# A decoder layer on one core: M's load on another queue, a new order inside the DeltaNet heads, later conditioning sums

## The chip, the cores and the metric

The kernel runs on 1 core of one Trainium2 chip. The metric is the device time of that core in microseconds (us). Names of the engines: PE is TensorE (matmuls; PEld its weight loads), DVE is VectorE, ACT is ScalarE, POOL is GpSimd, SP is SyncE. Each engine works through its own instructions in order, and they meet through semaphores. SP, ACT and POOL also issue DMA transfers, each in its own order.

## What is computed

One layer of a decoder over 1024 positions of width 1024, all in fp32. A conditioning vector `c` gives six vectors by one product with `w_ada`; a projection feeds sliding-window attention (16 query heads, 4 key heads, window 128, sinks) and a gated DeltaNet (8 heads of 128) in parallel. Both are gated, merged and projected, and a squared-ReLU MLP of width 4096 follows.

```python
mod = c_act @ w_ada[l] + b_ada[l]
sh1, sc1, gt1, sh2, sc2, gt2 = jnp.split(mod[:, None, :], 6, axis=-1)
u = x * (1.0 + sc1) + sh1
proj = u @ w_in[l]
qa, ka, va, dq, dk, dv, z, b_raw, a_raw, g_a, g_b = _split_in(proj)
y_a = _sliding_window_attention(qa, ka, va, sinks[l]) @ w_oa[l]
y_b = _gated_deltanet(dq, dk, dv, z, b_raw, a_raw, conv_w[l], a_log[l], dt_bias[l], dn_norm_w[l]) @ w_ob[l]
mixed = (jax.nn.sigmoid(g_a) * y_a + jax.nn.sigmoid(g_b) * y_b) @ w_out[l]
x = _layer_norm(ALPHA * x + (1.0 + gt1) * mixed, ln1_g[l], ln1_b[l])
u2 = x * (1.0 + sc2) + sh2
h = jnp.square(jax.nn.relu(u2 @ w_ff1[l] + b_ff1[l]))
x = _layer_norm(ALPHA * x + (1.0 + gt2) * (h @ w_ff2[l] + b_ff2[l]), ln2_g[l], ln2_b[l])
```

Inside a DeltaNet head the state goes from chunk to chunk (with `o` divided by its RMS and multiplied with `silu(z)` at the end; q, k and v first pass a convolution of 4 taps and a silu):

```python
v_new = u_c - jnp.einsum('bhck,bhkv->bhcv', w_c, state)
o_c = jnp.einsum('bhck,bhkv->bhcv', q_c, state) + jnp.einsum('bhcs,bhsv->bhcv', intra_c, v_new)
state = state * last_c[..., None, None] + jnp.einsum('bhck,bhcv->bhkv', k_c, v_new)
```

The triangular system of each chunk of 64 (`I + L`, one for every head and chunk, 128 in all) is the matrix M of the kernel.

## The kernel before

**The stream.** Almost all time is one stream of matmuls of 128x512 on PE. An fp32 product is made of three products of fp32r parts: high by high, high by low, low by high. `split_s` makes the parts: ACT copies the high part (L215), DVE subtracts it to get the low part (L216). `stream_unit` computes 128 output columns for all 1024 positions: 2 halves of 8 k tiles of 3 products, 48 matmuls (L248). Each takes one *position*, and `count[0]` is the current one.

**What sets the order.** Everything else is tied to positions by hand: `at(p, f)` puts an event into a heap and `after(n, f)` puts it n positions on; before each matmul of the stream `run_events` fires what is due. An event may issue a matmul, a DVE or ACT instruction or a DMA. So PE, DVE and ACT run in exactly the order of these numbers. The DMA issues of SP and POOL are placed by the same events, but their order within these two queues is set by a scheduler from what the transfers wait for.

**Stage b** is 26 units (keys, queries, gates) up to position Q0 = 1248. The 64 attention slots run in it: `att_scores` (L803, L804) multiplies the queries `qs` with the keys `khh` and `kll`. `k_parts` makes those: ACT copies a half tile (L747), DVE subtracts (L752), and each half is copied to the other 64 partitions by a DMA of POOL's queue (L748, L753). In the same stage DVE solves the triangular systems. They come from DRAM as M, 2 MB (L683, on POOL's queue, issued ahead of the keys' copies); `solve_init` (L686) sets the diagonal at position SOL0, and 124 steps (L701, L706) are spread up to SOL1 = 1150.

**The head stage** has 8 heads of 144 positions, each with a unit for q, for v and for z. After the unit of q or v, ACT copies the product to `pad` (L952) and scales it (L953), DVE adds three taps (L956) and ACT applies the silu (L961). A unit of z ends in two silus to `sz` (L1202). The recurrence of a head runs beside the next head's units, eight chunks n = 0 to 7, in hops of 6 positions: `hd_a` (PE L1127, then DVE rhs L1129), `hd_b` (PE L1137, then ACT vn L1139), `hd_c` (PE L1147, then DVE St L1152; PE L1160, then ACT Square L1163 and DVE o copy L1164). After it `hd_norm` takes the Sqrt on ACT (L1172) and scales the eight chunks of o, and `hd_out` transposes them and multiplies with `sz` (L1192). E products (L1101) and v products (L1115, L1119) of a head are made ahead of its recurrence, which starts at R = b + 140, b being the head's first position (b + 168 for head 7).

**The conditioning sums.** The remaining four vectors of `mod` are made by DVE from 68 loads of 256 KB or a row of the bias, `ada_load`, issued on SP; `ada_add` (L993, L995) adds each to an accumulator, and `ada_part` closes each of the 8 sums with matmuls.

**Then** the attention output is loaded (`attn_load`) and split (`attn_split`) during the last unit of z, two projections with their gates follow (`ya_done` takes the sigmoid of a gate tile), the output mix (L1469), the layer norm, and the MLP (L1840, L1900).

## Time and profile before

| | |
|---|---|
| median of 3 runs (lowest to highest) | 1851.2 us (1850.14 to 1852.37) |
| the profiled execution | 1854.92 us, span 1853.2 us |
| granted clock of the profiled execution | 0.992 |
| busy share PE / PEld / DVE / ACT / POOL | 98 / 81 / 69 / 55 / 17 % |
| DMA, mean over the span | 182 GB/s |

The profiled execution is one run, 3.7 us above the median; a sum made from its rows stands against its own time. In rows of the profile a line number leads to the code above, `x` is a count, and what stands in brackets is the idle time of the engine just before the instruction with what ended it. A window row has a stretch, its length, each engine's busy time, the granted clock of PE (1.00 is full), the share of the DMA engines and GB/s. A busy PE is not a PE at full rate: matmuls of 0.39 us overlap, one starting every 0.23 us.

### The profile page before, as it was taken

The numbers are of one execution on the slowest core, as the hardware profiler recorded it, in microseconds if no ns is written. First come the engines' busy times: TensorE is split into PE (matmuls) and PEld (weight loads), VectorE is DVE, ScalarE is ACT, GpSimd is POOL, SyncE is SP. The second block draws the span as 40 slices with busy tenths as digits, with TensorE's granted clock in tenths as the row PEclk, the third lists the DMA queues.
The fourth block names the chain that finished last, engine by engine and source line by source line (L and its number), as shares of the span: only waits on it lengthen the run. The fifth ranks groups of instructions, "written<-read, shape, count | busy, mean of one in ns | idle before, by whom it ended". The sixth has DMA issues, their size and how long they took to land.

```text
span 1853.2 us, 26168 instructions
## 1 busy us (share of the span) xinstructions
PE 1817.6 (98%) x9161; PEld 1505.5 (81%) x9161; DVE 1281.0 (69%) x2405; ACT 1022.8 (55%) x2297; POOL 314.4 (17%) x465
## 2 busy tenths in 40 slices
PE   8999999999999999999999999999999999999997
PEld 6977788888887888888878888877788887888886
DVE  6687588988855666666554445788767676576697
ACT  4698578888874454554554322465555555434341
POOL 0233233444331000000001110002212120000000
PEclk8999999999999999999999999999999999999999
DMA  9655622232257454444445644359887879755571
GB/s 276 200 199 202 197 89 85 61 99 80 81 195 203 144 154 136 141 143 139 119 156 199 192 153 151 117 169 314 306 277 264 268 250 389 274 183 182 199 256 46
DMA packets 262670, 337.74 MB, mean 182 GB/s; under 512 B 26261, under 2 KB 171366, under 8 KB 262282
## 3 DMA queue, kind: packets, MB, share of 16 engines
q1 hardware_dynamic: 223210, 212.94, 36.5%
q0 software_dynamic: 31328, 108.44, 17.4%
q10 hardware_dynamic: 8000, 14.68, 2.2%
q8 instruction: 72, 1.18, 0.2%
q14 instruction: 60, 0.49, 0.1%
HBM read 231.40 MB, written 102.51 MB: 180 GB/s over the span
## 4 chain that ended last, share of the span: by engine, by line
PE 80%; DVE 6%; ACT 4%; DMA 4%; issue 2%; POOL 0%; SPq 0%; ACTq 0%; DVEq 0%; POOLq 0%
PE mm L248 34%; PE mm L1840 7%; PE mm L1900 6%; PE b L1900 4%; PE a L1900 4%; PE b L1840 3%; PE a L1840 2%; PE mm L1469 2%; PE c L1900 2%; PE c L878 1%; PE a L1469 1%; PE mm L188 1%; PE mm L187 1%; PE mm L186 1%; PE a L1137 1%
## 5 line engine op out<-in xcount | busy, mean ns | idle before, releaser
L248 PE MATMUL mm<-uh,wl 128*128 128x512 f32 x800 | 332.7, 416 | 0.0
L248 PE MATMUL mm<-ul,wh 128*128 128x512 f32 x800 | 322.2, 403 | 0.0
L248 PE MATMUL mm<-uh,wh 128*128 128x512 f32 x800 | 319.0, 399 | 0.0
L216 DVE TENSOR_TENSOR sp<-sraw,sp 128x1024 fp32r<-128x1024 f32 x112 | 132.8, 1220 | 77.3 <-ACT sp L215 77.2
L215 ACT ACTIVATE sp<-sraw 128x1024 fp32r<-128x1024 f32 x112 | 112.7, 1054 | 123.0 <-PE b L1900 75.4
L248 PEld LDWEIGHTS mm<-ul,wh 128*128 128x128 f32 x800 | 151.6, 189 | 26.6 <-issue 0.2
L248 PEld LDWEIGHTS mm<-uh,wl 128*128 128x128 f32 x800 | 152.2, 190 | 23.1 <-issue 4.0
L248 PEld LDWEIGHTS mm<-uh,wh 128*128 128x128 f32 x800 | 152.4, 191 | 21.5 <-issue 0.2
L1900 PE MATMUL mm<-sp 128*128 128x512 f32 x528 | 136.9, 390 | 1.1 <-DVE sp L216 1.1
L1900 PEld LDWEIGHTS mm<-sp 128*128 128x128 f32 x528 | 98.5, 188 | 22.0 <-DVE sp L216 1.8
L216 DVE TENSOR_TENSOR wl<-wr,wh 128x1024 fp32r<-128x1024 f32 x81 | 99.9, 1234 | 8.9 <-ACT wh L215 8.8
L215 ACT ACTIVATE wh<-wr 128x1024 fp32r<-128x1024 f32 x81 | 85.1, 1051 | 21.4 <-PE c L1469 14.1
L1900 PE MATMUL a<-sp 128*128 128x512 f32 x336 | 92.6, 390 | 0.0
L1139 ACT ACTIVATE vn<-a,brk 128x128 f32<-128x128 f32 x64 | 23.5, 367 | 108.4 <-PE a L1137 107.4
L1900 PE MATMUL b<-sp 128*128 128x512 f32 (+1 forms) x336 | 80.0, 374 | 0.0
L811 DVE CUSTOM_DVE_ANT_0 nscore<-a,amask,nsink 128x256 f32<-128x256 f32 (+1 forms) x128 | 54.6, 464 | 36.5 <-PE a L804 35.8
L863 POOL TENSOR_SCALAR_AFFINE_SELECT pl<-ph 128x512 fp32r<-128x512 f32 x56 | 64.6, 1154 | 76.3 <-DVE ph L856 59.0
L1900 PEld LDWEIGHTS a<-sp 128*128 128x128 f32 x336 | 63.1, 188 | 13.1
L1900 PEld LDWEIGHTS b<-sp 128*128 128x128 f32 x336 | 60.5, 188 | 11.2
L216 DVE TENSOR_TENSOR wl<-fraw,wh 128x1024 fp32r<-128x1024 f32 x43 | 52.6, 1223 | 22.7 <-ACT wh L215 22.4
L822 POOL TENSOR_TENSOR sm<-sm 128x256 f32<-128x256 f32 x56 | 48.5, 866 | 95.7 <-ACT sm L818 53.1
L818 ACT ACTIVATE sm<-nscore,stat 128x257 f32<-128x257 f32 (+1 forms) x128 | 61.9, 486 | 2.7 <-DVE stat L811 2.5
(522 smaller groups left out, 4654.9 us busy)
## 6 DMA issues: line engine op xcount, KB each, us to landing
wr<-in_w_in_dram SPq DMA_DIRECT2D x60, 512.0 KB, 3.6
sraw<-hf_d SPq DMA_DIRECT2D x54, 512.0 KB, 4.3
adaw<-in_w_ada_dram SPq DMA_DIRECT2D x73, 256.0 KB, 4.6
fraw<-in_w_ff_dram SPq DMA_DIRECT2D x32, 512.0 KB, 5.5
sraw<-wt_d SPq DMA_DIRECT2D x32, 512.0 KB, 4.5
hf_d<-t ACTq DMA_DIRECT2D x48, 256.0 KB, 4.0
wt_d<-wx POOLq DMA_DIRECT2D x48, 256.0 KB, 3.0
sraw<-in_w_ff_dram SPq DMA_DIRECT2D x22, 512.0 KB, 5.5
```

The source lines that it names most:

```text
L186: T.matmul(t, lhsT=wh[:, k, :], rhs=xh[k][:, sl], start=k == 0, stop=False)
L215: A.activation(out=hi, in_=src, func=AF.Copy)
L216: after(lag, lambda: V.tensor_tensor(out=lo, in0=src, in1=hi.bitcast(F32), op=ALU.subtract))
L248: T.matmul(ts[half], lhsT=w[:, k, :], rhs=xx[k][:, sl], start=k == 0 and m == 0, stop=k == KT - 1 and m == 2)
L811: V.tensor_tensor_reduce(out=ns[:, i, 1:1 + W], in0=sc[:, i * 2 * P:i * 2 * P + W], in1=amask[:, mo:mo + W], scale=-1.0, scalar=nsink[:, 2 ...
L818: A.activation(out=sm[:, i, 0:1 + W], in_=ns[:, i, 0:1 + W], func=AF.Exp, scale=-1.0, bias=st[:, i:i + 1], accum_out=st[:, 2 + i:3 + i])
L822: G.tensor_tensor(out=sm[:, :, 1 + P:1 + 2 * P], in0=sm[:, :, 1:1 + P], in1=sm[:, :, 1 + P:1 + 2 * P], op=ALU.add)
L863: G.affine_select(out=flat4(part), in_=flat4(full), pattern=[[0, 4], [1 if odd else -1, P]], compare_op=ALU.is_ge if odd else ALU.is_gt, f ...
L1139: after(1, lambda: A.activation(out=vn, in_=Wp[:, 0:P], func=AF.Copy, scale=brk[:, n, h:h + 1]))
L1469: T.matmul(pt, lhsT=m[k][:, tok], rhs=w[:, k % 2, :], start=k == 0 and w is wh and m is mh, stop=k == KT - 1 and m is ml)
L1840: T.matmul(pt, lhsT=a[:, k0 + k, :], rhs=b[k], start=begin and k == 0 and x_ == 0, stop=k == 3 and x_ == 2, skip_group_check=True)
L1900: T.matmul(to, lhsT=a[:, f, t * P:(t + 1) * P], rhs=b[:, f, lo:up], start=(begin or own) and s % NS == 0 and f == 0 and x_ == 0, stop=s % ...
```

## The change

It has these parts.

1. M is loaded by a DMA of ACT's queue, issued 18 positions after the key unit's end, instead of POOL's queue ahead of the keys' copies. The solve starts at position 192 instead of 164 and ends at 1150 as before.
2. Conditioning item i is loaded at Q0 + 170 + 13 i instead of Q0 + 21 + 14 i, added 28 positions later instead of 21, and the sums of the last four close at +35 instead of +28. The first three loads still leave SP ahead of the head's loads.
3. In the head stage the taps and their silu come one position later; the copy of o on DVE comes 9 positions after its hop instead of 4 (the Square stays at 4); odd chunks of o are scaled on ACT in all heads instead of only the last; the norm of heads 0 to 5 comes 2 positions after the recurrence instead of 8, with `hd_out` at +18 and +21 instead of +19 and +24 after it; head 6's `hd_out` moves to +25 and +36. In head 0 the transposes of q and v come 10 and 8 positions later.
4. Three of the eight attention splits move by 4 to 12 positions, behind the last unit's two silus. The first gate's sigmoid comes 38 positions after its load instead of 20.

```diff
@@ -680,7 +680,9 @@
...
     Mf = M.rearrange("p s c -> p (s c)")
-    nc.gpsimd.dma_start(out=Mf, in_=md_d.rearrange("h b n s c -> (h b n) (s c)"))
+
+    def solve_load():
+        nc.scalar.dma_start(out=Mf, in_=md_d.rearrange("h b n s c -> (h b n) (s c)"))
 
@@ -714,7 +716,7 @@
...
 
-    SOL0, SOL1 = 164, 1150
+    SOL0, SOL1 = 192, 1150
     cost = [s * (63 - s) + 80 for s in range(1, 63)]
@@ -908,6 +910,7 @@
...
     at(KEY0 + 17, k_parts, 0, 1)
+    at(KEY0 + 18, solve_load)
     at(max(slot(15) + 1, 48 * (units_b.index(("k", 1)) + 1) + 4), k_parts, 1, 0)
@@ -957,8 +960,8 @@
...
             for j in range(3):
-                after(4 + 4 * j, tap, 2 - j)
-            after(16, lambda: A.activation(out=dst[:, sl], in_=dst[:, sl], func=AF.Silu))
+                after(5 + 4 * j, tap, 2 - j)
+            after(17, lambda: A.activation(out=dst[:, sl], in_=dst[:, sl], func=AF.Silu))
         return done
@@ -981,11 +984,11 @@
...
             nc.sync.dma_start(out=w, in_=w_ada[k * P:(k + 1) * P, lo:lo + HALF])
-            after(21, ada_add, w, k)
+            after(28, ada_add, w, k)
         else:
...
         if k == KT - 1 + (f < 4):
-            after(28, ada_part, f, w[0:1, :])
+            after(28 if f < 4 else 35, ada_part, f, w[0:1, :])
 
@@ -1024,7 +1027,7 @@
...
     for i, (f, k) in enumerate(items):
-        at(Q0 + 21 + 14 * i, ada_load, i, f, k)
+        at(Q0 + 170 + 13 * i, ada_load, i, f, k)
 
@@ -1159,10 +1162,8 @@
...
 
-        def put():
-            A.activation(out=junk(), in_=op_[:, 0:P], func=AF.Square, accum_out=d["sso"][:, n:n + 1])
-            V.tensor_copy(out=d["o"][:, cs], in_=op_[:, 0:P])
-        after(4, put)
+        after(4, lambda: A.activation(out=junk(), in_=op_[:, 0:P], func=AF.Square, accum_out=d["sso"][:, n:n + 1]))
+        after(9, lambda: V.tensor_copy(out=d["o"][:, cs], in_=op_[:, 0:P]))
 
@@ -1174,7 +1175,7 @@
...
                 V.reciprocal(out=fs, in_=fs)
-            if h == 7 and n % 2:
+            if n % 2:
                 A.activation(out=d["o"][:, chunk(n)], in_=d["o"][:, chunk(n)], func=AF.Copy, scale=fs[:, n:n + 1])
@@ -1208,9 +1209,9 @@
...
         for half in range(2):
-            at(b + 58 + 24 * half, hd_qturn, h, half)
+            at(b + (58 if h else 68) + 24 * half, hd_qturn, h, half)
             at(max(b + 64, late + 40) + 24 * half, hd_kq, h, half)
-            at(b + 98 + 24 * half, hd_vturn, h, half)
+            at(b + (98 if h else 106) + 24 * half, hd_vturn, h, half)
         at(max(b + 70, late + 50), hd_z, h)
@@ -1218,10 +1219,10 @@
...
             at(R + 3 * HOP * n + 2 * HOP, hd_c, h, n)
-        late = R + 3 * HOP * NT + (14 if h == 6 else 8)
+        late = R + 3 * HOP * NT + (14 if h == 6 else 8 if h == 7 else 2)
         at(late, hd_norm, h)
-        at(late + 19, hd_out, h, 0)
-        at(late + 24, hd_out, h, 1)
+        at(late + (25 if h == 6 else 19 if h == 7 else 18), hd_out, h, 0)
+        at(late + (36 if h == 6 else 24 if h == 7 else 21), hd_out, h, 1)
 
@@ -1245,14 +1246,14 @@
...
                 at(count[0] + (0, 0, 0, 26, 36, 32, 38, 44)[k], attn_load, k)
-                at(count[0] + (8, 14, 20, 38, 43, 50, 56, 62)[k], attn_split, k)
+                at(count[0] + (8, 14, 20, 38, 55, 50, 60, 66)[k], attn_split, k)
         stream_unit(uh, ul, sz_done(h), interleave=h == 7)
...
         nc.gpsimd.dma_start(out=t, in_=ga_d[f])
-        after(20, lambda: A.activation(out=t, in_=t, func=AF.Sigmoid))
+        after(20 if f else 38, lambda: A.activation(out=t, in_=t, func=AF.Sigmoid))
 
```

How this moves instructions, at three places. In the rows a line number of the changed kernel is up to 3 above that of the kernel before.

The first is the start of attention on POOL's queue, before and after. M is the matrix of systems, khh and kll are the keys' parts.

```order
L599 DMA e_d<-e 128x1024
L683 DMA M<-md_d 128x4096
L748 DMA khh<-khh 64x512
L753 DMA kll<-kll 64x512
L748 DMA khh<-khh 64x512
```

```order
L599 DMA e_d<-e 128x1024
L750 DMA khh<-khh 64x512
L755 DMA kll<-kll 64x512
L750 DMA khh<-khh 64x512
L755 DMA kll<-kll 64x512
```

The keys' copies now follow the last store directly; the load of M (L685) stands on ACT, behind the third copy of khh (L749) and ahead of a weight split (L215) and the fourth copy.

The second is the hop n = 2 on DVE, here that of head 2, from the state St to the next rhs, before and after. `ada` is the conditioning accumulator, `wl` a weight's low part, `sz` the product of `hd_out`.

```order
L1152 SCALAR_TENSOR_TENSOR St<-St,last,a 128x128
L956 SCALAR_TENSOR_TENSOR qT<-pad,convc,qT 128x512
L995 SCALAR_TENSOR_TENSOR ada<-ada,c_col 128x512
L216 TENSOR_TENSOR wl<-wr,wh 128x1024
L1164 COPY o<-c 128x128
L1192 SCALAR_TENSOR_TENSOR sz<-b,convc,sz 128x512
L956 SCALAR_TENSOR_TENSOR qT<-pad,convc,qT 128x512
L1129 SCALAR_TENSOR_TENSOR rhs<-a,negegc,vr 128x128
```

```order
L998 SCALAR_TENSOR_TENSOR ada<-adaw,c_col,ada 128x512
L1155 SCALAR_TENSOR_TENSOR St<-St,last,a 128x128
L216 TENSOR_TENSOR wl<-wr,wh 128x1024
L959 SCALAR_TENSOR_TENSOR qT<-pad,convc,qT 128x512
L1132 SCALAR_TENSOR_TENSOR rhs<-a,negegc,vr 128x128
L959 SCALAR_TENSOR_TENSOR qT<-pad,convc,qT 128x512
```

One tap, the conditioning add, the copy of o and the product to `sz` no longer stand between St and rhs.

The third is the boundary between two heads on ACT, here from head 1 to head 2: Square of the last chunk (`junk,sso`), silu of the second half of `sz`, vn of the next head's first chunk, and the Sqrt of the norm (`fs`), before and after.

```order
L1163 ACTIVATE junk,sso<-c 128x128
L1202 ACTIVATE sz<-mm 128x512
L1139 ACTIVATE vn<-a,brk 128x128
L1172 ACT_TABLE_LOAD
L1172 ACTIVATE fs<-fs,eps_q 128x8
L1163 ACTIVATE junk,sso<-c 128x128
L1139 ACTIVATE vn<-a,brk 128x128
```

```order
L1165 ACTIVATE junk,sso<-c 128x128
L1173 ACT_TABLE_LOAD
L1173 ACTIVATE fs<-fs,eps_q 128x8
L1203 ACT_TABLE_LOAD
L1203 ACTIVATE sz<-mm 128x512
L1142 ACTIVATE vn<-a,brk 128x128
L1179 ACTIVATE o<-o,fs 128x128 x4
L1165 ACTIVATE junk,sso<-c 128x128
L1142 ACTIVATE vn<-a,brk 128x128
```

The Sqrt with its table load, and a second table load for the silu, now stand ahead of the silu and of vn; the table load that the next silu needed before (at L961, a few rows on) is gone. Four scalings of o follow vn.

## The prediction

> **What bounds the kernel now.** I read the page first: who is busy, and what the chain that ended last is made of.
>
> ```profile
> PE 1817.6 (98%) x9161; PEld 1505.5 (81%) x9161; DVE 1281.0 (69%) x2405; ACT 1022.8 (55%) x2297; POOL 314.4 (17%) x465
> PE 80%; DVE 6%; ACT 4%; DMA 4%; issue 2%; POOL 0%; SPq 0%; ACTq 0%; DVEq 0%; POOLq 0%
> ```
>
> PE is busy for 98% of the span. The change removes no matmul, so it can only win what PE loses by standing still or by running at a lower clock. The next view is the list of PE's waits: who waits, for whom, then us in total, times, longest.
>
> ```profile
> PE a L1137 <- DVE rhs L1129: 4.2, 7, 1.0
> PE b L1115 <- DVE E L1101: 2.4, 1, 2.4
> PE a L803 <- DMA M<-md_d: 2.3, 1, 2.3
> ```
>
> These three are the longest in the list and all lie in code that the diff touches. Two are a single wait each, so I looked at the granted clock around them (stretch: its length, busy time of PE, PEld, DVE, ACT, POOL, then clock, DMA share, GB/s).
>
> ```profile
> 226.20:229.00 2.80, 0.51 (x3) 0.12 (x2) 0.75 (x4) 0.00 (x0) 0.42 (x1) 1.00 1.39 226
> 230.70:234.20 3.50, 3.50 (x10) 2.73 (x9) 3.33 (x11) 1.25 (x4) 0.00 (x0) 0.51 0.84 201
> 575.50:578.40 2.90, 0.48 (x4) 0.09 (x2) 2.61 (x7) 1.16 (x3) 0.00 (x0) 1.00 1.12 268
> 578.90:582.40 3.50, 3.50 (x11) 2.74 (x10) 1.51 (x3) 1.85 (x6) 0.56 (x1) 0.52 0.99 224
> 1303.50:1305.40 1.90, 0.43 (x2) 0.00 (x1) 0.00 (x0) 0.60 (x2) 0.00 (x0) 1.00 0.84 326
> ```
>
> Each of the two long gaps (2.3 and 2.4 us idle) is followed, some 2 us and 0.5 us later, by 3.5 us at a clock of 0.51 and 0.52: 3.5 × 0.49 = 1.7 us of work lost each time. The gap of 1.5 us at 1303.5 leaves no such mark in its own stretch. I charge both stretches to their gaps.
>
> A gap costs a little more than its idle time, because matmuls of the stream overlap:
>
> ```profile
> 692.69 0.40 PE L248 MATMUL mm<-ul,wh 128*128 128x512 f32 x1
> 692.92 0.39 PE L1147 MATMUL a<-vn,kd 128*128 128x128 f32 x2
> ...
> 226.25 0.39 PE L248 MATMUL mm<-uh,wh 128*128 128x512 f32 x1
> 228.93 0.30 PE L803 MATMUL a<-khh,qs 128*128 128x128 f32 x1 [2.29 <-DMA M<-md_d]
> ```
>
> A matmul of 0.40 is followed by the next start after 0.23. At 226.25 the next comes after 2.68, so 2.45 is lost where 2.29 is shown idle: 0.16 more per gap.
>
> **Edit 1, M's load.** The wait at 228.93 is put down to M, but the first score matmul reads khh, kll and qs. Its half copies khh and kll go out on POOL's queue behind M.
>
> ```profile
> 216.81 0.55 POOL L683 DMA_DIRECT2D M<-md_d  x1 [7.74 <-DVE kll L752]
> ...
> M<-md_d POOLq DMA_DIRECT2D x1, 2048.0 KB, 11.2
> khh<-khh POOLq DMA_DIRECT2D x4, 128.0 KB, 11.8
> ...
> DMA to landing us min/median/max: 2.2/2.4/3.1
> ...
> 228.16 0.11 DVE L686 MEMSET M<- 128x64 f32 x1 [5.39 <-DMA M<-md_d]
> ```
>
> M takes 11.2 us from issue to landing; a khh copy behind it takes 11.8 at the median, and the four later ones (second row of landings, of the tile khh from 300 to 480 us) 2.4. With M on ACT's queue after the third khh copy, the copies go out at about 217 and would land some 3 to 6 us later, before 226.5. The gap goes: −2.45, and with it its half-clock stretch, −1.7; together **−4.1**. ACT pays one issue, priced by this row:
>
> ```profile
> 1283.02 0.33 ACTq L1553 DMA_DIRECT2D hf_d<-t  x1
> ```
>
> It stands ahead of a weight split and the last khh copy; 0.33 late is covered by ACT's slack there (in the 2.80 us stretch at 226.20 ACT ran nothing). What is late next is M: issued near 217 it lands at 228.2 by its own 11.2. The solve's memset now stands 28 positions later (28 × 0.23 = 6.4 us), near 228.8 in a stream without the gap, behind the first score's maximum on DVE. If M were as slow as the slowest load below (14.7), DVE would stand until 231.8, and everything queued behind the memset with it: the first attention slots' maxima, then PE. Bounds of this edit: −4.1 and 0 (the wait only changes its name). I take −4.1, nearer to M's own row. The solve has 28 of 986 positions less; DVE is 69% busy, so at nothing.
>
> **Edit 2, the conditioning sums.** The wait at 578 has this history (first row from the chain of waits, second from DVE's timeline):
>
> ```profile
> 561.03 14.73 DMA ada<-in_w_ada_dram
> ...
> 577.12 1.12 DVE L1101 SCALAR_TENSOR_TENSOR E<-b,rk,E 128x128 f32<-128x128 f32 x4
> ```
>
> A conditioning load of 256 KB lands 14.7 us after issue, because it shares the queues with the head loads; the add waits for it on DVE, the E products stand behind the add, and PE's L1115 waits for those. Loads from the fourth on now come 149 positions (34 us) later, after the head loads, and their adds 28 instead of 21 positions behind. The wait goes: 2.42 + 0.16 = −2.6, and −1.7 for the clock: **−4.3**; bounds −4.3 and −2.6, or 0 if another load there is as late. What is given back is below, since all 68 items now end at Q0 + 170 + 13 × 67 = Q0 + 1041, close to the last head.
>
> **Edit 3, the hop that waits.** All seven waits of L1137 are the same hop, n = 2 of heads 0 to 6. This is the one of head 2 (DVE's timeline, then PE's):
>
> ```profile
> 698.85 0.35 DVE L1152 SCALAR_TENSOR_TENSOR St<-St,last,a 128x128 f32<-128x128 f32 x1 [0.16 <-PE a L1147]
> 699.37 0.75 DVE L956 SCALAR_TENSOR_TENSOR qT<-pad,convc,qT 128x512 f32<-128x512 f32 x1 [0.17 <-ACT qT L953]
> 700.04 0.75 DVE L995 SCALAR_TENSOR_TENSOR ada<-ada,c_col 128x512 f32<-128x512 f32 x1
> 700.70 1.22 DVE L216 TENSOR_TENSOR wl<-wr,wh 128x1024 fp32r<-128x1024 f32 x1
> 701.84 0.29 DVE L1164 COPY o<-c 128x128 f32<-128x128 f32 x1
> 702.04 0.74 DVE L1192 SCALAR_TENSOR_TENSOR sz<-b,convc,sz 128x512 f32<-128x512 f32 x1
> 702.70 0.74 DVE L956 SCALAR_TENSOR_TENSOR qT<-pad,convc,qT 128x512 f32<-128x512 f32 x1
> 703.36 0.35 DVE L1129 SCALAR_TENSOR_TENSOR rhs<-a,negegc,vr 128x128 f32<-128x128 f32 x1
> ...
> 703.76 0.49 PE L1137 MATMUL a<-rhs,TT 128*128 128x128 f32 x2 [1.04 <-DVE rhs L1129]
> ```
>
> Between St and rhs DVE is 4.51 us on work of others, and PE waits 1.04. After the change only the weight subtraction (start to start 1.14) and one tap (0.66) stand between them: the conditioning add (0.66), the o copy (0.20), the gated product (0.66) and one tap have moved elsewhere. That is 0.52 + 1.14 + 0.66 = 2.3 us, 2.2 less where 1.04 was short; the other six hops lack the add and have more room. All seven go: 4.2 + 7 × 0.16 = −5.3. The pieces land in neighbouring hops; counted over the new order with these durations the fullest of these holds 2.9 us, and hops with 3.1 run without a wait today. I take **−5.2**; bounds −5.3 and 0 (work merely moved).
>
> **Edit 4, the last head and the attention splits.**
>
> ```profile
> 939.12 1.15 ACT L215 ACTIVATE ah<-ar 128x512 fp32r<-128x512 f32 x2 [2.19 <-DMA ar<-attn_d]
> 940.17 1.07 ACT L1202 ACTIVATE sz<-mm 128x512 f32<-128x512 f32 x2
> ...
> 940.80 0.50 PE L248 MATMUL mm<-ah,wh 128*128 128x512 f32 x1 [1.29 <-ACT sz L1202]
> 951.09 0.49 PE L1147 MATMUL a<-vn,kd 128*128 128x128 f32 x2 [0.60 <-ACT vn L1139]
> ```
>
> PE waits for the silu because two ah copies that wait for their load stand before it; after the change the silu stands first. That wait goes: −1.29 − 0.16 = −1.45. The one at 951 and two of 0.3 to 0.4 behind it keep most of their cause: ACT has the same copies plus four scalings there. I take **−2.0**; bounds −1 and −3.2 (all four).
>
> **What is given back.** Six head boundaries (heads 0 to 5) get a longer chain on ACT: last Square, table load, Sqrt, table load, silu of the second sz half, then vn, for which PE waits. Before, the Sqrt came behind vn:
>
> ```profile
> 688.91 0.20 ACT L1163 ACTIVATION_READ_ACCUMULATOR junk<-c 128x1 f32 x1
> 691.05 0.60 ACT L1202 ACTIVATE sz<-mm 128x512 f32<-128x512 f32 x1 [1.95 <-PE mm L248]
> 691.80 0.37 ACT L1139 ACTIVATE vn<-a,brk 128x128 f32<-128x128 f32 x1
> 692.18 1.28 ACT L1172 ACT_TABLE_LOAD   x1
> 693.48 0.30 ACT L1172 ACTIVATE fs<-fs,eps_q 128x8 f32<-128x8 f32 x1
> ```
>
> The Square ends at 689.11 and PE's L1147 starts without a wait at 692.92 (its row is above): 3.81 us. The chain is 1.30 + 0.30 + 1.30 + 0.60 + 0.37 = 3.87, so 0.06 per head. If the second load starts only with the silu's input (691.05), vn ends at 691.05 + 1.30 + 0.60 + 0.37 = 693.32: 0.40 per head, 2.4 in all. I take **+0.4**, between them but near the first, because the load at 692.18 began without waiting for the Sqrt's input. The Trainium skill speaks against this edit: "ScalarE: Activation LUTs", section "What ACT_TABLE_LOAD costs", gives about 1.28 us for a load and 1.38 more for a drain at each switch; the trace agrees on 1.28, but its Sqrt starts 0.02 us behind its load, so the drain isn't seen here.
>
> The rest, **+0.7** (0 to +2.5): the conditioning sums now run beside the last heads and the attention loads, whose buffers come free only when the sums end, and the gate's sigmoid is moved; the nearest rows are waits of 0.3 to 1.3 at single places.
>
> **The sum.** −4.1 − 4.3 − 5.2 − 2.0 + 0.4 + 0.7 = −14.5 from the profiled execution's own 1854.9 us, so 1840.4. That execution lies 3.7 us above the median of the runs (1851.2), which I take to stay with the profile: **1836.7 us**. If every loss named here went and nothing came back it would be −4.1 − 4.3 − 5.3 − 3.2 = −16.9, or 1834.3.
>
> **Rivals.** *The half-clock stretches are not the gaps'.* At 1303.5 a gap has none, and one comes 2 us behind its gap. Then both stay somewhere: +3.4, 1840.1. The Trainium skill leans this way ("TensorE: Matmul & The Clock Gate", "What's actually happening"): the clock falls after an idle window of about 3.4 us, and no gap here is that long. Against it: both stretches follow the two longest gaps.
>
> *M lands late.* With 14.7 instead of 11.2 us the memset blocks DVE to 231.8 and the first slots lose about what edit 1 won: 1836.7 + 4.1 = 1840.8.
>
> *The stall only moves.* The o copies, taps and scalings taken out of n = 2 fill a neighbouring hop, or the adds at every 13th position drift into one: the waits stay at their 5.2, 1841.9; with edit 4 gone too, 1843.9.
>
> *Slower: ACT's chain at the head boundary.* It pays if it runs past its 3.81 us by more than 14.9/6 = 2.5 us per head, that is from 6.3 us on. That needs each of the two loads to take 1.25 more than its row. With a drain of the skill's size the chain would be 6.6 us, an estimate from that page, and the time 1853. By the rows alone: if both loads waited behind the silu's input at 691.05 the chain ended at 694.9, 2.0 late, 12 us in all: 1848.3. Rows speak against both.
>
> **How the numbers follow.** Forecast 0.62; clock 0.10; M late 0.10; stall moves 0.13; slower chain 0.05. Two runs of this kernel can be told apart from about 0.2% (3.7 us) on. All but the last and the worst of the stall case end below 1847.5: faster 0.91, same 0.05, slower 0.04. The range reaches from just under the floor, 1833.5, to the stall case with edit 4 gone, 1844.
>
> **What would show it.** Right: no wait at the first score and khh landing in 3 to 6 us; no half clock at 230 and 579; L1137's counterpart gone from the waits; ACT's Square-to-vn chain near 3.9 us with two loads in it. Wrong: a DVE wait for M of over 2 us, half clock elsewhere, a new entry of several times in PE's waits for rhs, vn or St.

## The result, and the profile after

The changed kernel takes 1837.51 us (median of 4 runs, 1837.03 to 1838.41) where the kernel before took 1850.97 beside it: a ratio of 0.9928, with a 95% interval of 0.9917 to 0.9940. Measured a second time on another chip it took 1837.84 against 1851.87, 0.9920 (0.9907 to 0.9934). The gain is 13 to 14 us, and 1836.7 had been forecast. One execution of all that follow, the profiled one of the first run of experiment 3, took 1995.5 us at a granted clock of 0.85, where the others lie at 0.99 and above, and is left out everywhere.

The profiled execution is 1837.18 us (span 1835.5). Its head:

```profile
PE 1812.4 (99%) x9160; PEld 1503.9 (82%) x9161; DVE 1276.9 (70%) x2377; ACT 1030.5 (56%) x2325; POOL 314.9 (17%) x464
PE 85%; DVE 5%; ACT 3%; DMA 3%; issue 1%; POOL 0%; ACTq 0%; DVEq 0%; POOLq 0%
```

PE's busy time fell by 5.2 us and its idle time by 12.5; the chain that ended last is 85% PE, where it was 80%. The list of PE's waits (who, for whom: us in total, times, longest) begins like this now:

```profile
PE warm L294 <- DVE wz L289: 1.7, 1, 1.7
PE b L1379 <- ACT rawu L1382: 1.6, 3, 1.0
PE a L331 <- DMA adaw<-in_w_ada_dram: 1.4, 3, 0.7
```

These three are in the program's start and between the output mix and the MLP, which the change leaves alone. No wait for rhs, E, M, sz, vn or St is left anywhere in the list. The two places with half clock are clean (windows: length, busy PE, PEld, DVE, ACT, POOL, clock, DMA share, GB/s):

```profile
224.00:230.00 6.00, 6.00 (x30) 5.04 (x29) 2.46 (x13) 1.46 (x6) 0.00 (x0) 1.00 1.36 231
230.00:234.00 4.00, 4.00 (x22) 3.32 (x22) 3.46 (x11) 3.03 (x8) 1.04 (x1) 1.00 0.61 219
565.00:575.00 10.00, 10.00 (x66) 8.30 (x65) 6.25 (x12) 5.18 (x18) 1.17 (x2) 1.00 1.16 277
575.00:582.00 7.00, 7.00 (x34) 5.78 (x34) 1.23 (x1) 3.00 (x7) 0.00 (x0) 1.00 0.65 185
```

At the first score M's load and the keys' copies now look like this (ACT's and POOL's timelines, PE's first score, DVE's memset, then a DMA row with KB and median us from issue to landing, and the landings of kll):

```profile
214.70 0.35 ACTq L685 DMA_DIRECT2D M<-md_d  x1
...
215.55 0.54 POOL L750 DMA_DIRECT2D khh<-khh  x1 [6.98 <-ACT khh L749]
217.56 0.53 POOL L755 DMA_DIRECT2D kll<-kll  x1 [1.48 <-DVE kll L754]
...
225.96 0.22 PE L805 MATMUL a<-khh,qs 128*128 128x128 f32 x1
...
227.20 0.11 DVE L688 MEMSET M<- 128x64 f32 x1
...
khh<-khh POOLq DMA_DIRECT2D x4, 128.0 KB, 9.4
...
DMA to landing us min/median/max: 8.3/9.2/9.7
```

PE and DVE wait for nothing here, but only just: the first kll copy, issued at 217.56, landed 8.3 us later, near 225.9, and PE's first product with kll started at 226.02. That copy left only 0.3 us earlier than in the kernel before (217.88 there) and landed 3.2 us earlier, since it took 8.3 us instead of 11.2; the first khh copy left 1.8 us earlier and took 9.9 instead of 11.2. What moved most is M itself. It was issued at 214.70 instead of 216.81, and by the trace's record of DMA packets its 2 MB ran from 215.7 to 224.3 us, before from 218.1 to 226.7. In both kernels the copies land behind M's last packet.

The hop n = 2 of head 2 on DVE:

```profile
687.79 0.35 DVE L1155 SCALAR_TENSOR_TENSOR St<-St,last,a 128x128 f32<-128x128 f32 x1 [0.66 <-PE a L1150]
688.06 1.22 DVE L216 TENSOR_TENSOR wl<-wr,wh 128x1024 fp32r<-128x1024 f32 x1
689.19 0.75 DVE L959 SCALAR_TENSOR_TENSOR qT<-pad,convc,qT 128x512 f32<-128x512 f32 x1
689.86 0.35 DVE L1132 SCALAR_TENSOR_TENSOR rhs<-a,negegc,vr 128x128 f32<-128x128 f32 x1
```

From St to rhs it takes 2.07 us where it took 4.51. And the boundary of two heads on ACT:

```profile
677.28 0.19 ACT L1165 ACTIVATION_READ_ACCUMULATOR junk<-c 128x1 f32 x1
677.49 1.28 ACT L1173 ACT_TABLE_LOAD   x1
678.78 0.30 ACT L1173 ACTIVATE fs<-fs,eps_q 128x8 f32<-128x8 f32 x1
679.10 1.28 ACT L1203 ACT_TABLE_LOAD   x1
680.39 0.60 ACT L1203 ACTIVATE sz<-mm 128x512 f32<-128x512 f32 x1
680.89 0.36 ACT L1142 ACTIVATE vn<-a,brk 128x128 f32<-128x128 f32 x1
...
681.05 0.39 PE L248 MATMUL mm<-ul,wh 128*128 128x512 f32 x1
681.30 0.49 PE L1150 MATMUL a<-vn,kd 128*128 128x128 f32 x2
...
681.77 0.48 PE L248 MATMUL mm<-uh,wl 128*128 128x512 f32 x1
```

From the Square's end (677.47) to PE's start 3.83 us pass; vn ends at 681.25 and PE starts 0.05 later. No wait is listed there, but vn is a little late: from the matmul of the stream ahead of L1150 to the one behind it pass 0.72 us, where the kernel before has 0.59. The same 0.12 is lost at five of the six boundaries of heads 0 to 5, 0.6 us in all.

**Where the time went.** Every 48th matmul of the stream (L248) can be set against the same one of the kernel before, by its start in the two traces:

| matmul of L248 | start before | start after | ahead by |
|---|---|---|---|
| 1 | 174.82 | 174.30 | 0.52 |
| 145, before the first score | 217.41 | 216.89 | 0.52 |
| 289, behind it | 260.19 | 255.46 | 4.73 |
| 433 | 304.06 | 298.86 | 5.21 |
| 1249, head 0 begins | 548.59 | 543.78 | 4.80 |
| 1381, behind the E products | 588.69 | 579.58 | 9.11 |
| 2401, the last unit | 938.67 | 924.01 | 14.66 |
| 2449 | 955.47 | 937.21 | 18.26 |
| 3121 | 1116.60 | 1098.34 | 18.26 |

The span ends 17.7 us earlier, so 0.5 is lost again behind the stream, mostly in the MLP. The medians differ by 13.5 only; that gap of 4 us is taken up below.

### The profile page after: what moved, and what is told of

Its sections match the earlier page's. It is cut to its first block, busy times and chain, and to the rows that moved or that the text cites. A ratio compares the mean times of both kernels' runs of the same rounds, so it can differ in the third digit from the quotient of the medians.

```text
span 1835.5 us, 26166 instructions
## 1 busy us (share of the span) xinstructions
PE 1812.4 (99%) x9160; PEld 1503.9 (82%) x9161; DVE 1276.9 (70%) x2377; ACT 1030.5 (56%) x2325; POOL 314.9 (17%) x464
## 4 chain that ended last, share of the span: by engine, by line
PE 85%; DVE 5%; ACT 3%; DMA 3%; issue 1%; POOL 0%; ACTq 0%; DVEq 0%; POOLq 0%
PE mm L248 40%; PE mm L1841 6%; PE mm L1901 6%; PE b L1901 4%; PE a L1901 4%; PE b L1841 3%; PE c L1901 2%; PE a L1841 2%; PE mm L1470 2%; PE c L880 2%; PE mm L188 1%; PE mm L187 1%; PE mm L186 1%; PE a L1470 1%; DMA sraw<-in_w_ff_dram 1%
## 5 line engine op out<-in xcount | busy, mean ns | idle before, releaser
L248 PE MATMUL mm<-uh,wl 128*128 128x512 f32 x800 | 330.5, 413 | 0.0
L248 PE MATMUL mm<-ul,wh 128*128 128x512 f32 x800 | 321.0, 401 | 0.0
L248 PE MATMUL mm<-uh,wh 128*128 128x512 f32 x800 | 317.0, 396 | 0.0
L215 ACT ACTIVATE sp<-sraw 128x1024 fp32r<-128x1024 f32 x112 | 112.7, 1054 | 122.6 <-PE b L1901 75.3
L248 PEld LDWEIGHTS mm<-ul,wh 128*128 128x128 f32 x800 | 150.5, 188 | 26.5 <-issue 0.2
L248 PEld LDWEIGHTS mm<-uh,wl 128*128 128x128 f32 x800 | 151.4, 189 | 23.2 <-issue 4.0
L248 PEld LDWEIGHTS mm<-uh,wh 128*128 128x128 f32 x800 | 151.5, 189 | 21.5 <-issue 0.2
L1901 PE MATMUL mm<-sp 128*128 128x512 f32 x528 | 136.8, 390 | 0.8 <-DVE sp L216 0.8
L1901 PEld LDWEIGHTS mm<-sp 128*128 128x128 f32 x528 | 98.5, 188 | 21.7 <-DVE sp L216 1.7
L215 ACT ACTIVATE wh<-wr 128x1024 fp32r<-128x1024 f32 x81 | 85.1, 1051 | 21.4 <-PE c L1470 13.9
L1901 PE MATMUL a<-sp 128*128 128x512 f32 x336 | 92.5, 389 | 0.0
L1901 PE MATMUL b<-sp 128*128 128x512 f32 (+1 forms) x336 | 80.0, 374 | 0.0
L1901 PEld LDWEIGHTS a<-sp 128*128 128x128 f32 x336 | 63.1, 188 | 13.1
L1901 PEld LDWEIGHTS b<-sp 128*128 128x128 f32 x336 | 60.5, 188 | 11.2
L215 ACT ACTIVATE wh<-fraw 128x1024 fp32r<-128x1024 f32 x43 | 45.0, 1056 | 33.2 <-PE b L1841 16.3
```

What stands on the lines that cost most here:

```text
L215: A.activation(out=hi, in_=src, func=AF.Copy)
L248: T.matmul(ts[half], lhsT=w[:, k, :], rhs=xx[k][:, sl], start=k == 0 and m == 0, stop=k == KT - 1 and m == 2)
L1901: T.matmul(to, lhsT=a[:, f, t * P:(t + 1) * P], rhs=b[:, f, lo:up], start=(begin or own) and s % NS == 0 and f == 0 and x_ == 0, stop=s % ...
```

## The experiments

**1. M's load put back.**

```diff
-        nc.scalar.dma_start(out=Mf, ...)      # at KEY0 + 18
+    nc.gpsimd.dma_start(out=Mf, ...)          # ahead of the keys' copies
-    SOL0, SOL1 = 192, 1150
+    SOL0, SOL1 = 164, 1150
```

> The changed kernel with M's load back on POOL's queue ahead of the keys' copies, and the solve from position 164. My theory (the first score waited for key copies behind M, and the half-clock stretch hangs on that gap): a wait of about 2.3 us at the first score, a stretch of about 3.5 us at half clock within some us behind it, and the kernel slower by 3 to 4.3 us. Rival (the half clock has nothing to do with the gap): the wait comes back without the stretch, slower by 2.5 us. Rival (the gap was there for another cause): same time as the changed kernel within 1 us.

Measured: 1843.18 us, ratio to the kernel before 0.9960 (0.9945 to 0.9974), 5.7 above the changed kernel's median. The gap and the stretch are both there (PE's timeline, then a window):

```profile
228.09 0.30 PE L804 MATMUL a<-khh,qs 128*128 128x128 f32 x1 [2.29 <-issue]
...
229.00:232.50 3.50, 3.50 (x12) 2.73 (x11) 3.36 (x9) 0.60 (x1) 0.00 (x0) 0.60 0.83 162
```

At this place the kernel falls 4.1 us behind the changed one, and 0.5 more at matmul 433, as in the table above. So the first theory holds here. The profiled execution also has a wait of 2.9 us in the MLP (end of this section), which no edit touched.

**2. M's load alone.** The kernel before with this edit (the Square and the copy of o become two events at one position, which leaves ACT's order as it was):

```diff
-    nc.gpsimd.dma_start(out=Mf, ...)          # ahead of the keys' copies
+        nc.scalar.dma_start(out=Mf, ...)      # at KEY0 + 18
-    SOL0, SOL1 = 164, 1150
+    SOL0, SOL1 = 192, 1150
```

> The kernel before with only M's load on ACT's queue and the solve from position 192. My theory (this part pays by itself: the gap of 2.3 us and its half-clock stretch): faster than the kernel before by 2.5 to 4.2 us, no wait at the first score, the waits of the head stage as before. Rival (M's later landing stalls DVE and takes the gain back): a wait of DVE for M of over 2 us, and 0 to 1.5 us faster.

Measured: 1849.87 against 1851.87, ratio 0.9987 (0.9975 to 0.9998). The wait at the first score is gone, DVE's memset runs at 227.50 without a wait, and the stream gains 4.1 us on the kernel before at that place and 4.6 by matmul 433. The time of the medians, 2.0 less, is under what was expected, though the interval reaches to 4.6; its executions spread from 1846.8 to 1855.0. M landing late, the second of the rivals of the prediction, is not seen in any run. The run also shows a gap of 1.9 us at the E products, from 571.5 to 573.4, without half clock behind it. The two stretches below meet inside the gap; why they are cut there is said under "Half clock belongs to the gaps".

```profile
569.47:572.88 3.41, 2.04 (x22) 1.37 (x18) 2.04 (x5) 0.59 (x2) 0.62 (x1) 1.00 1.06 364
572.88:576.29 3.41, 2.85 (x15) 2.46 (x16) 2.25 (x5) 2.90 (x9) 0.56 (x1) 1.00 1.14 201
```

**3. The conditioning sums put back.**

```diff
-        at(Q0 + 170 + 13 * i, ada_load, i, f, k)     # ada_add 28 later, ada_part 28 or 35
+        at(Q0 + 21 + 14 * i, ada_load, i, f, k)      # ada_add 21 later, ada_part 28
```

> The changed kernel with the conditioning sums at their old places (loads from Q0 + 21, every 14 positions, added 21 behind). My theory: the late load at Q0 comes back and with it one wait of about 2.4 us behind the E products and perhaps its half-clock stretch: slower by 2.5 to 4.3 us; no wait of rhs comes back, since a hop with one conditioning add holds 2.8 us of DVE work in the new order where 3.6 and more stalled. Rival (the sums' phase is what freed the recurrence): two waits of rhs at heads 2 and 5 besides, of some 0.5 to 1 us each, slower by 4 to 6.5 us.

Measured: 1845.16 us, 0.9962 (0.9951 to 0.9974). This run left no profile that can be read beside the others, so the kernel ran once more:

> The changed kernel with the conditioning sums at their old places, once more, since the profiled execution of the first time was disturbed. As before: a wait of some 2.4 us of PE for the E products near position 1248 + 48 + 48, with a half-clock stretch behind it; no waits of rhs; slower by 2.5 to 4.3 us. Rival: waits of rhs at heads 2 and 5, or a new wait at another place that the old sums meet in the new order; the time of the first runs (7 us slower) speaks for something more than 4.3.

Measured: 1844.37 us, 0.9955 (0.9942 to 0.9967), 6.5 above the changed kernel beside it (1837.84). The longest wait that the changed kernel did not have, and what stands ahead of it on DVE:

```profile
PE b L1071 <- DVE E L1104: 4.6, 1, 4.6
...
570.78 0.75 DVE L998 SCALAR_TENSOR_TENSOR ada<-ada,c_col 128x512 f32<-128x512 f32 x1 [3.91 <-DMA ada<-in_w_ada_dram]
571.45 0.75 DVE L959 SCALAR_TENSOR_TENSOR vT<-pad,convc,vT 128x512 f32<-128x512 f32 x1
572.11 1.12 DVE L1104 SCALAR_TENSOR_TENSOR E<-b,rk,E 128x128 f32<-128x128 f32 x4
```

The mechanism is the one of the prediction: DVE stands in an add whose load is late, and E with it. The size was missed: in the new order of head 0 the first matmul behind is another one (L1071, earlier than L1118), and it waits 4.6 us, not 2.4; with the half clock behind it the stream loses 6.2 there. No wait for rhs came back, so the rival that the sums' phase freed the recurrence falls.

**4. The head stage's order put back** (taps, copy of o, scalings, norm, outputs, head 0's transposes), the rest as changed.

```diff
-                after(5 + 4 * j, tap, 2 - j)                  # silu 17
+                after(4 + 4 * j, tap, 2 - j)                  # silu 16
-        after(9, lambda: V.tensor_copy(out=d["o"][:, cs], ...))
+        after(4, lambda: V.tensor_copy(out=d["o"][:, cs], ...))
-            if n % 2:
+            if h == 7 and n % 2:
-    late = ... 14 if h == 6 else 8 if h == 7 else 2          # outputs +25/+36, +19/+24, +18/+21
+    late = ... 14 if h == 6 else 8                            # outputs +19/+24
-    at(b + (58 if h else 68) + 24 * half, hd_qturn, h, half)  # hd_vturn 98 if h else 106
+    at(b + 58 + 24 * half, hd_qturn, h, half)                 # hd_vturn 98
```

> The changed kernel with the head stage's order of before (taps and silu one position earlier, copy of o at +4, o scaled on DVE but for head 7, norm at +8 with its outputs, head 0's transposes), and M, sums and last splits as changed. My theory (DVE work between St and rhs at n = 2 is the cause, the sums' add only adds to it): seven waits of rhs come back, 0.37 to 0.53 us each without the add, about 2.9 us of waits and 0.16 more for each, slower by 3.9 us; one table load per head boundary is gone from ahead of vn and wins nothing (0 to 0.4). Rival (the sums' phase alone freed the hops): no waits of rhs, 0. Rival (the double table load costs): the kernel gets faster in these places, a gain of up to 2.4 us against the 3.9.

Measured: 1841.67 us, 0.9946 (0.9930 to 0.9963), 4.2 above the changed kernel.

```profile
PE a L1140 <- DVE rhs L1132: 2.9, 7, 0.5
...
PE b L1190 <- DVE o L1181: 1.1, 1, 1.1
```

Seven waits of 2.9 us in all, as expected to the tenth; in the stream the kernel loses 0.5 to 0.7 at each of the seven heads, 4.4 together, and another 1.5 in the last unit, where head 6's outputs now wait for their o. So of the 5.5 us gained over the head stage about 4.4 are the order's. The rest fits the two conditioning adds that stood in the hops of heads 2 and 5: PE waited 1.04 us in each of these before, and 0.53 and 0.38 here.

**5. The last splits put back** (positions of three attention splits, and the first gate's sigmoid).

```diff
-                at(count[0] + (8, 14, 20, 38, 55, 50, 60, 66)[k], attn_split, k)
+                at(count[0] + (8, 14, 20, 38, 43, 50, 56, 62)[k], attn_split, k)
-        after(20 if f else 38, ...)
+        after(20, ...)
```

> The changed kernel with the attention splits at the positions of before (so that two splits stand ahead of the last silus on ACT) and the first gate's sigmoid at +20. My theory: PE waits again for the silu of sz in the last unit, 1.3 us and 0.16, and perhaps for vn behind it (0.6): slower by 1.5 to 2.5 us. Rival (the later sums or the new order set this place, not the splits): same within 0.5 us.

Measured: 1841.30 us, 0.9947 (0.9932 to 0.9962), 3.8 above; the stream loses 4.8 in the last unit. The theory named vn only in passing and the scaled o not at all; the rival, no more than 0.5 us, is out by the time. PE's two new waits, the stretch around them, and ACT's rows ahead of them:

```profile
PE b L1190 <- ACT o L1179: 1.7, 1, 1.7
...
PE a L1150 <- ACT vn L1142: 1.2, 1, 1.2
...
932.00:940.00 8.00, 5.06 (x20) 3.72 (x18) 2.08 (x3) 4.56 (x10) 0.00 (x0) 0.79 0.23 74
...
931.49 1.28 ACT L1256 ACT_TABLE_LOAD   x1 [1.94 <-DMA ga<-ga_d]
932.78 1.06 ACT L1256 ACTIVATE ga<-ga 128x1024 f32<-128x1024 f32 x1
933.75 1.26 ACT L1179 ACTIVATE o<-o,fs 128x128 f32<-128x128 f32 x4
```

What stands ahead of o and vn is not a split but the first gate's sigmoid, back at 20 positions: ACT waits 1.94 us for the gate's load, takes 1.28 for a table load and 1.06 for the sigmoid, and only then comes to the scalings of o, half of which the new order has on ACT, and to vn. Half clock follows. So the half of this edit that costs is the sigmoid's, by the trace; no run puts back the splits alone. PE does not wait for sz here, although two more split copies stand ahead of it again: ACT's last wait for a split's load ended at 920.91, 2.6 us ahead of the silus, where in the kernel before it ended 1.05 us ahead of them. The old positions fit the new order worse than they fitted the old one: undoing one part costs more than this part brought.

**6. The norm put back** for heads 0 to 5 (one table load at the boundary, behind vn) with its outputs.

```diff
-    late = ... 14 if h == 6 else 8 if h == 7 else 2          # outputs +25/+36, +19/+24, +18/+21
+    late = ... 14 if h == 6 else 8                            # outputs +19/+24
```

> The changed kernel with the norm of heads 0 to 5 at +8 and the outputs at +19 and +24, as before (one table load of the head boundary behind vn, the gated product of hd_out back between St and rhs at n = 2). My theory (the pair of table loads is hidden to the last tenth, and the hop has 0.8 us of slack of which the product takes 0.66): no wait of vn or rhs, same as the changed kernel within 0.7 us. Rival (the product alone is what stalled): up to six waits of rhs, slower by 1 to 3 us. Rival (the pair costs): faster by 0.4 to 2.4 us.

Measured: 1839.68 us (1835.72 to 1841.72), 0.9922 (0.9902 to 0.9942), not to be told from the changed kernel. No wait for vn or rhs is in its list; the last unit has a wait of 1.0 us for head 6's o, whose outputs were moved back too. The times cannot tell what the pair of table loads costs, but the trace can. At the boundary of the rows of the result (head 1 to head 2) PE now has this:

```profile
681.66 0.40 PE L248 MATMUL mm<-ul,wh 128*128 128x512 f32 x1
681.89 0.39 PE L1150 MATMUL a<-vn,kd 128*128 128x128 f32 x2
...
682.25 0.48 PE L248 MATMUL mm<-uh,wl 128*128 128x512 f32 x1
```

Here 0.59 us pass between the two matmuls of the stream, 0.72 in the changed kernel, and 0.59 to 0.60 at all six boundaries. With the loads behind vn the 0.12 is gone, so the pair costs 0.12 at five boundaries, 0.6 us in all.

**7. Three copies more in the chain ahead of vn.**

```diff
+        for _ in range(3 if h < 6 else 0):
+            A.activation(out=junk(), in_=ident, func=AF.Copy)
         A.activation(out=fs, in_=fs, func=AF.Sqrt, ...)
```

> The changed kernel with three more copies of 128x128 on ACT ahead of the Sqrt in the norm of heads 0 to 5 (results used by no one), some 0.6 us more in the chain from the last Square to vn. My theory (after the change this chain ends just as PE asks for vn, with no slack): PE waits for vn six times, 0.4 to 0.6 us each, and the kernel is slower by 6 x (0.5 + 0.16) = 4 us at most, 3 to 4. Rival (there is slack of some tenths, or the chain begins later than PE's need): 0 to 1.5 us.

Measured: 1842.26 us (1840.05 to 1843.42), 0.9937 (0.9921 to 0.9953): 4.7 above by the medians, but 1.7 to 3.1 above by the ratios of the two measurements of the changed kernel, which did not run beside it.

```profile
678.76 0.70 ACT L1174 ACTIVATE junk<-ident 128x128 f32<-128x128 f32 x3
...
683.29 0.49 PE L1150 MATMUL a<-vn,kd 128*128 128x128 f32 x2 [0.47 <-ACT vn L1142]
```

The chain from the Square's end to vn's end is 4.38 us here and 3.78 in the changed kernel, 0.60 more. PE waits 0.47, and at five of the six boundaries the stream loses 0.6 (3.1 in all). So the changed kernel's chain has nothing to spare, as the theory said: the slower rival of the prediction had its mechanism right, and every tenth that the chain grows is paid.

**8. A longer gap at the first score**, by one more copy of 1 MB ahead of M on POOL's queue (experiment 1 besides).

```diff
+    nc.gpsimd.dma_start(out=t_d[...][:, 0:2048], in_=md_d[...][:, 0:2048])
```

> The changed kernel with M's load back on POOL's queue, the solve from position 164, and behind the keys' back a further copy of 1 MB of the same data (DRAM to DRAM, used by no one) issued ahead of M, so that the keys' copies land still later: a gap of some 5 to 8 us at the first score instead of 2.3. My theory (a gap of 2.3 us falls into half clock by chance, a gap clearly above 3.5 us does so always): a stretch at half clock directly behind the gap, in the profile and in all executions, so that their spread is no more than that of the changed kernel (some 1.5 us) but for other gaps; slower than the changed kernel by the gap and 0.16 and 1.7. Rival (chance at any length): no stretch in the profile, or executions in two groups 1.7 us apart.

Measured: 1842.62 us (1841.39 to 1848.09), 0.9938 (0.9920 to 0.9956). The copy was issued at 216.46 and landed 5.6 us later; M, issued at 217.26, took 10.6 us behind it instead of 11.1 in experiment 1, and the gap stayed at 2.5 us, with half clock behind it, so the question it was made for is not answered. Another gap answered something: a load of T was late (2.8 us of wait at L1061, from 567.3 to 570.1), and no half clock followed.

```profile
565.19:568.60 3.41, 2.12 (x13) 1.39 (x11) 0.94 (x4) 2.48 (x11) 0.00 (x0) 1.00 1.05 324
568.60:572.01 3.41, 1.92 (x20) 1.66 (x21) 3.34 (x6) 1.22 (x3) 0.00 (x0) 1.00 1.08 189
572.01:575.43 3.42, 3.42 (x21) 2.98 (x20) 0.46 (x1) 0.64 (x1) 0.00 (x0) 1.00 1.05 372
```

**9. Both kernels once more, unchanged**, for what a profiled execution is worth.

> The kernel before, unchanged, for another profiled execution. My theory after the first runs (the kernel before's executions lie near 1850.3, 1852.5, 1853.8 and 1855.3, steps of about 1.7 us, so the half-clock stretches come in some executions only): an execution near 1850.3 shows the gaps of 2.3 and 2.4 us at 226 and 575, and no half-clock stretch behind them; one near 1855 shows both. Rival (each long gap always brings its stretch, as the sum of the prediction has it): both stretches in every execution, whatever its time.

> The kernel before, a third profiled execution. The two so far (1854.9 and 1856.2 us) lie 4 to 5 us above the medians and both show the gaps of 2.3 to 2.8 us at 226 and 575 with a half-clock stretch behind each. My theory (the lengths of these two gaps, set by landings of transfers, and their stretches vary from execution to execution, 0 to 4 us each): an execution near 1850 has shorter gaps or lacks a stretch, one near 1855 looks like the first two. Rival (the gaps and stretches are the same in every execution, and the difference lies elsewhere, as in the MLP's waits): both gaps and stretches as before even at 1850, and some other wait shorter.

> The changed kernel, unchanged, for another profiled execution and more times beside those of the kernel before on one chip. Theory one (the profiled execution of the kernel before lies 3.7 us above its median because of the two half-clock stretches that most of its executions do not have): the changed kernel has neither gap, so its profiled execution lies within 1.5 us of its median, and its executions spread less than those before (1848 to 1857). Theory two (a profiled execution is a slow one for any kernel): it lies 3 to 5 us above its median here too. The gain of the medians should again be 0.7%, 13 us.

The kernel before: profiled executions of 1856.2 and 1853.56 us, among runs with medians of 1851.26 and 1852.97. Both show both gaps (2.6 and 2.8 us; 2.2 and 2.4) and a half-clock stretch behind each, just as the first (2.3 and 2.4); the stretch behind the gap of 2.8 is twice as long as the others. So the theory that most executions lack the stretches is not borne out, though no execution near 1850 was caught in a profile. The changed kernel: profiled at 1837.12 with a median of 1837.84 (1837.12 to 1838.88). A profiled execution is not a slow one in general.

**A wait that comes and goes.** The MLP's code is the same in all these kernels, but a wait of L1901 for a split weight (`ACT sp L215`), at about 1530 us, is in some profiles (2.9 us in experiment 1, 2.6 in the second run of 3, 2.3 in 8, 1.1 in two parts in 7, 1.0 in 2, with half clock behind all but the last) and not in the three of the kernel before, the two of the changed one, nor in experiments 4, 5 and 6. It can put some 4 us on top of what an edit costs at its own place, and does so in the time of experiment 1's profiled execution. What decides it was not settled.

## Why the prediction was right, point by point

| term of the sum | predicted | in the profile |
|---|---|---|
| M's load | −4.1 | −4.2 at the first score, −0.5 more by matmul 433 |
| conditioning sums | −4.3 | −4.3 |
| the hop n = 2 | −5.2 | −6.1 (−5.5 over the head stage, with the next but one row) |
| last head and splits | −2.0 | −3.6 |
| two table loads ahead of vn | +0.4 | +0.6 |
| the rest | +0.7 | +0.4 in stage b, −0.5 at the start, +0.5 behind the stream |
| sum | −14.5 | −17.7 |
| the profiled execution's place over the median | stays at +3.7 | −0.3, and −0.7 the second time |

The hop's 6.1 is what the stream's matmuls on both sides of the seven late L1137 show, 0.65 to 1.31 us each. That is 0.27 more than each listed wait, where the prediction added 0.16.

**The causes of the three long waits hold.** The first score waited for key copies behind M (experiments 1 and 2), the E products for an add behind a late load (3), and the hop for DVE work between St and rhs (4).

**How the first wait went was foreseen only in part.** The prediction let the copies go out at about 217 and land 3 to 6 us later, and named that as a sign of being right. They took 8.3 to 9.9 us and landed behind M's last packet, as before. They were in time by less than 0.2 us (experiment 2 and both profiles of the changed kernel), with M's packets through 2.4 us sooner. So the term of −4.1 is right with a landing that was mis-sized, and that it came out whole is partly luck. No run separates M's earlier issue from its other queue.

**Half clock belongs to the gaps.** That it would stay was the first rival. It went with both gaps in the changed kernel, and came back with each gap that was put back. It is not a certainty of a gap, though: behind 12 of the 13 gaps of 2.2 us and more named here it came, behind the one of 2.8 in experiment 8 it did not, nor behind the single ones of 1.6 (kernel before) and 1.9 (experiment 2).

The traces show what decides. In the 13 profiles used here the granted clock changes only at multiples of 3.413 us, counted from its first change, within 3 ns over the whole span. Cut at these multiples, 13 intervals (from 60 us on, without the last 10 us of a span) leave PE idle for 1.63 us or more, and behind every one the clock stood at half for the next interval. Of the intervals at full clock with less idle time one was followed by half clock (1.49 us, experiment 7). Here are the interval with the least idle time among the 13 and the one just below it, both of the kernel before:

```profile
227.30:230.72 3.42, 1.79 (x10) 1.60 (x11) 2.37 (x8) 0.00 (x0) 0.52 (x1) 1.00 1.39 234
...
1302.50:1305.92 3.42, 1.81 (x9) 1.19 (x8) 0.00 (x0) 1.12 (x2) 0.00 (x0) 1.00 0.82 317
```

The first is followed by 3.41 us at 0.50, the second by full clock. A multiple that falls inside a gap divides it: the 2.8 us of experiment 8 became 1.29 and 1.49, the 1.9 us of experiment 2 became 1.36 and 0.55, and neither brought half clock. So the prediction's charge of one stretch for each gap held for these two gaps in all three profiles of the kernel before (one of the six stretches is two intervals long), and hung on where the multiples fell. The Trainium skill ("TensorE: Matmul & The Clock Gate", "What's actually happening") sets an idle window of about 3.4 us before the clock falls; the length of the interval agrees, but here some 1.6 us of idle time in it were enough.

**The last head was sized wrong.** The gain of 3.6 lies outside the bounds that the prediction set for this term (1 to 3.2). The step that failed is "the one at 951 and two of 0.3 to 0.4 behind it keep most of their cause: ACT has the same copies plus four scalings there". The copies are not what made vn late: all 16 of them (two for each split) stand ahead of vn on ACT in both kernels. What stood between them and vn was the first gate's sigmoid, which the change moves behind vn (ACT's rows before, then after):

```profile
947.48 1.28 ACT L1255 ACT_TABLE_LOAD   x1 [1.50 <-issue]
948.78 1.06 ACT L1255 ACTIVATE ga<-ga 128x1024 f32<-128x1024 f32 x1
...
932.64 0.35 ACT L1142 ACTIVATE vn<-a,brk 128x128 f32<-128x128 f32 x1
933.00 1.28 ACT L1256 ACT_TABLE_LOAD   x1
```

In the changed kernel vn ends at 932.99 and the stream loses about 0.3 us there. Experiment 5 shows how much hangs on these positions: 4.8 us. It also shows that the wait for sz need not come back with its two copies ahead of it, since the loads land earlier in the new kernel; that the splits' new positions are what ended it is not shown.

**The table loads.** 0.06 or 0.40 us per head were the two prices; 0.12 at five of six boundaries was measured. The second load began at 679.10. In experiment 6, where the silu waits for its input, that comes 2.31 us after the Square's start (677.71 to 680.02), which in the changed kernel is 679.41. So the load did not wait for the silu's input, and the lower price was the nearer one. Both loads took 1.28 and were followed by their function after 0.01, without the drain that the Trainium skill names ("ScalarE: Activation LUTs", "What ACT_TABLE_LOAD costs").

**The step from profile to median failed, and hid the rest.** The sum was 3.2 us short of what the profile shows, and the assumption that the execution's 3.7 above the median would stay was 4 us off, the other way. The two cancel: that 1836.7 came within 1 us of 1837.5 is partly luck. A sum made right would have said 1837.2 for the profiled execution, and that offset would then have given 1833.5. Executions of the kernel before spread from 1848.0 to 1857.2 and its three profiled ones lie at 1853.6 to 1856.2; those of the changed kernel spread from 1837.0 to 1838.9. What spreads them is not settled. Waits that end with a transfer are the first candidates: experiment 4, without either of the two long gaps, spreads by 1.2 us (4 executions), and experiments 1 and 2, with one each, by 13 and 8 (10 and 11). But experiment 6, whose profile has no gap above 1.4 us behind the start, spreads by 6.0, and the second run of 3, with a gap of 4.6, by 1.3 only (4.6 the time before). Where the multiples of 3.413 us fall also differs from execution to execution; that this spreads the times was not tried.

**The rivals that did not come.** M was on time (experiment 2: no wait for it on DVE). No stall moved into another hop: the list of waits has none. The slower case needed 2.5 us more in the chain; experiment 7 shows that every tenth more is paid from the present length on.

## What to carry to other kernels

When one engine is 98% busy, list its waits, ask for each what stands ahead of the late instruction on its queue, and add the price of a stretch at a lower clock (1.7 us here) behind each gap of some 2 us, as a likely cost and not a certain one: here this gave the terms of the three longest waits to within 1 us at their places. Look at the rows between the instruction that seems to blame and the late one: the gate's sigmoid stood there, and the prediction blamed the copies. A list without waits does not show a loss of 0.12 us; the distance between the stream's matmuls does. A profiled execution of a kernel with waits for transfers can lie several us above its median, and that offset is part of what a change removes; do not carry it over. Parts of a reordering depend on one another: put back one by one, four parts cost 5.7, 6.5, 4.2 and 3.8 us, 20 in all, where together they brought 13.5. The wait in the MLP that comes and goes may be in some of these times; in the stream alone, by the traces, it is 22 against 17.7.

## What the hardware showed that was not expected

The clock's changes lie on a fixed raster of 3.413 us, and half clock came behind an interval of it with 1.63 us or more of idle time. That is also why two short gaps can bring it: the 1.7 and 1.2 us of experiment 5 lie in one interval (933.09 to 936.50, 2.32 us idle), where single gaps of 1.6 and 1.9 did not.

Copies of 128 KB landed behind a load of 2 MB whether it was on their queue or on another: 10.9 to 12.3 us right behind M on the same queue (the kernel before, experiment 1), 8.2 to 10.1 with M on ACT's and issued 2.1 us earlier (the changed kernel, experiment 2). An extra copy of 1 MB ahead of M did not lengthen the wait at the first score beyond the 2.2 to 2.6 us that it has without (experiment 8: 2.5).
